# GLA scores prepared two levels at a time, and four more visits ahead of the gate rows' transposes, in a hybrid encoder layer on one core

## Chip, cores and metric

The kernel runs on one core of one Trainium2 chip. The metric is device time in microseconds (us), the median of several runs. PE is TensorE (PEld its weight loads), DVE is VectorE, ACT is ScalarE, POOL is GpSimd, SP is the engine that issues nearly all DMAs.

## What is computed

One layer of an encoder over 1024 tokens of width 1024. Token mixing normalises the input, projects it once, and gives the columns to two groups of four heads: mLSTM heads and GLA heads (linear attention with a forget gate for every key dimension). Both are scanned forward and backward and added, normalised per head, gated, projected out, normalised and added to the input. Then comes a gated MLP with a depthwise convolution of width 3. Cut to the part that the change touches, GLA in one direction is:

```
b = jnp.cumsum(a_, axis=-2)
diff = b[..., :, None, :] - b[..., None, :, :]
decay = jnp.exp(jnp.where(causal, diff, -jnp.inf))
s = jnp.einsum('bhtd,bhsd,bhtsd->bhts', q_, k_, decay)
o = jnp.einsum('bhts,bhse->bhte', s, v_) + jnp.einsum('bhtd,bhde->bhte', q_ * jnp.exp(b), s_st)
```

The scores s of two tokens need the decay between them, key dimension by key dimension, so they are no plain product of queries and keys.

## The kernel before

**Stages.** The input x is normalised, transposed and split into two parts (xh, xl) whose products keep fp32 accuracy. A first piece of the input projection runs at once (L259). Then two Python generators are interleaved: proj(), the rest of the input projection, and mix(), everything of the mixers. After them come the output projection (oacc, L957), the MLP (pr, L1018) and its down projection (pr, L1176), the last two by a Strassen scheme.

**The order of the work.** _interleave holds a clock for each generator and always advances the one whose clock is lower, up to its next yield, a visit. A visit adds the generator's weight to its clock. proj has 0.25. mix sets its own weight as it goes: W_AUX 0.85 at first, W_GLA 0.19, W_ML 0.26, W_OUT 0.5. So the weights and the yields decide how much projection stands between two pieces of the mixers. A visit of proj is 12 matmuls of 256 columns (t_block, L180, tile tacc) or 6 of 512 (f_block, L169, tile facc); proj has 176 such visits and a few without matmuls. The compiler then puts each engine's instructions in an order of its own: it keeps this order as priority, and takes a later instruction first where it reckons that the earlier one would wait.

**mix, in its order.** gla_decay (8 matmuls z, L374, and the cumulative gate sums, stored in dS); gate_rows, a generator that works out the gates of the mLSTM heads on DVE and ACT and ends in transposes of gi, gf and rm (tile ptc, L367) behind its last yield; gla(); mlstm(); out_weights(). gla waits with empty visits until the projections that it needs are done (done["bq"], done["bv"]), mlstm likewise for "aqk" and "av". gla runs levels(0), then states (the carried states of all 8 chunks), then for each chunk levels of the next one and finish of this one.

**levels(c)** makes the scores of one chunk of 128 tokens. It works by halving: for L = 64, 32, 16, 8, 4, 2, 1 the pairs of tokens that lie in the two halves of a block of 2L are given a reference point at the middle, so that the decay splits into a factor for the query and one for the key. For one L: POOL subtracts the reference (Dt, L610), ACT takes two exponentials into PSUM (E, L614 and L615), DVE multiplies them with the queries (Q, L624) and the keys (K, L628, or L622 for 32; for 64 a single product, L618). Then it yields, and in the next visit TensorE multiplies keys and queries (tile sc: L633 and L634 for 64, L645 for 32, L647 for the others), and the scores are kept: copied on ACT into Pt for 64 and 32 (L635, L636, L651), into acc for 16 (L653), and by DVE's copy_predicated into acc for the rest (L655). The diagonal (L661) follows in the same visit as L = 1, and then the operands of finish. That is 8 yields a chunk. D, E and Q have two buffers each, the pool ps, from which sc, the transposes and o are taken, has three banks.

**finish(c)** multiplies scores with values and adds the product with the state (tile o, L677, L678), copies it out and takes the norms on ACT.

**mlstm** takes matmuls Um (L729), sr (L753) and nd (L773, L774); the last nd is the last matmul of the mixers.

**out_weights** begins when mlstm has given back its memory. It loads the output weights in eight pieces of 512 KB (oraw, L817) through three buffers, two of tag yv and one of tag gv; each is split by ACT (woh, L106) and DVE (wol, L107), with a yield behind each. Once the projection is done (done["gate"]) it calls prep(0): the loads yv and gv of the first 128 tokens into the same buffers, their scaling on DVE (L837), transposes (L843) and a split into yh and yl. The first output product (oacc, L957) needs the split weights and yh.

Of the kernel before, what the change touches and what calls it, by code (L numbers as in the profile page):

```python
# [9 lines left out]
F32 = mybir.dt.float32  # L10
F32R = mybir.dt.float32r
U32 = mybir.dt.uint32
AF = mybir.ActivationFunctionType
ALU = mybir.AluOpType
# [3 lines left out]
P = 128  # L18
# [5 lines left out]
H = 4  # L24
# [9 lines left out]
TEMP = 16.0  # L34
# [21 lines left out]
def tile_encoder_layer(  # L56
# [6 lines left out]
    nc = tc.nc  # L63
# [30 lines left out]
    ps = ps_ctx.enter_context(tc.tile_pool(name="ps", bufs=3, space=PSUM))  # L94
# [28 lines left out]
    # ------------------------------------------------------------------  # L123
    # normalised input, transposed and split
    # ------------------------------------------------------------------
# [33 lines left out]
    bmask = mid.tile([P, 5, 32], U32, name="bmask")  # L159
    # ------------------------------------------------------------------  # L160
    # input projection
    # ------------------------------------------------------------------
# [87 lines left out]
    for t in range(NT):  # L250
# [5 lines left out]
        acc = mm.tile([P, NS], F32, name="vacc", tag="mm")  # L256
# [3 lines left out]
        if t % 4 == 0:  # L260
            vst = stg.tile([P, 4, 256], F32, name="stg")
        nc.scalar.copy(out=sml[:, t, 0:96].rearrange("p (n r) -> p n r", n=3),
                       in_=acc[:, 256:288].rearrange("p (o r) -> p o r", o=1).broadcast_to([P, 3, 32]))
# [35 lines left out]
    def gate_rows():  # L299
# [7 lines left out]
        for i in range(2):  # L307
            rs = slice(32 * i, 32 * i + 4)
# [20 lines left out]
        for i in range(2):  # L329
            rs = slice(32 * i, 32 * i + 4)  # L330
# [6 lines left out]
        for i in range(2):  # L337
            rs = slice(32 * i, 32 * i + 4)
# [24 lines left out]
        yield  # L363
# [122 lines left out]
    # ------------------------------------------------------------------  # L486
    # mixers and the rest of the input projection
    # ------------------------------------------------------------------
    mctx = ExitStack()

    def mix():
# [49 lines left out]
        def gla():  # L541
# [51 lines left out]
            def levels(c):  # L593
# [11 lines left out]
                mi = 0  # L605
                for L in (64, 32, 16, 8, 4, 2, 1):
                    nb = P // (2 * L)
                    Dt = w2k("D")
                    xv = X.rearrange("p h (n j) -> p h n j", j=2 * L)
                    nc.gpsimd.tensor_tensor(out=Dt.rearrange("p h (n j) -> p h n j", j=2 * L), in0=xv,  # L610
                                            in1=xv[:, :, :, L:L + 1].broadcast_to([P, H, nb, 2 * L]), op=ALU.subtract)
                    E = pe.tile([P, H, P], F32, name="E", tag="pe")
                    half = lambda z, i: z.rearrange("p h (n i j) -> p (h n) i j", i=2, j=L)[:, :, i, :]
                    nc.scalar.activation(half(E, 0), half(Dt, 0), AF.Exp, scale=-1.0 / TEMP)  # L614
                    nc.scalar.activation(half(E, 1), half(Dt, 1), AF.Exp, scale=1.0 / TEMP)  # L615
                    Q = w2k("Q")
                    if L == 64:
                        nc.vector.tensor_tensor(out=Q, in0=E, in1=z64, op=ALU.mult)  # L618
                    elif L == 32:
                        nc.vector.tensor_tensor(out=Q, in0=E, in1=qq, op=ALU.mult)  # L620
                        K = w2k("K", 1)
                        nc.vector.tensor_tensor(out=K, in0=E, in1=kk, op=ALU.mult)  # L622
                    else:
                        nc.vector.tensor_tensor(out=Q, in0=E, in1=qq, op=ALU.mult)  # L624
                        K = kz[L]
                        for i in range(2):
                            rs = slice(64 * i, 64 * i + 64)
                            nc.vector.tensor_tensor(out=half(K[rs], i), in0=half(E[rs], i), in1=half(kk[rs], i), op=ALU.mult)  # L628
                    yield
                    if L == 64:  # L630
                        sc = ps.tile([P, H, 64], F32, name="sc", tag="ps")
                        for h in range(H):
                            nc.tensor.matmul(sc[0:64, h, :], Q[0:64, h, 0:64], Q[0:64, h, 64:128], start=True, stop=True)  # L633
                            nc.tensor.matmul(sc[64:128, h, :], Q[64:128, h, 64:128], Q[64:128, h, 0:64], start=True, stop=True)  # L634
                        nc.scalar.copy(out=Pt[0:64, :, 64:128], in_=sc[0:64])  # L635
                        nc.scalar.copy(out=Pt[64:128, :, 0:64], in_=sc[64:128])  # L636
                    else:
                        sc = ps.tile([P, H, 32], F32, name="sc", tag="ps")
                        for h in range(H):
                            for b in range(4):  # L640
                                bs = slice(32 * b, 32 * b + 32)
                                if L == 32:
                                    ob = slice(32 * (b ^ 1), 32 * (b ^ 1) + 32)
                                    rs = lo if b % 2 == 0 else hi
                                    nc.tensor.matmul(sc[bs, h, :], K[rs, h, bs], Q[rs, h, ob], start=True, stop=True)  # L645
                                else:
                                    nc.tensor.matmul(sc[bs, h, :], K[:, h, bs], Q[:, h, bs], start=True, stop=True)  # L647
                        if L == 32:
                            for b in range(4):
                                ob = slice(32 * (b ^ 1), 32 * (b ^ 1) + 32)  # L650
                                nc.scalar.copy(out=Pt[32 * b:32 * b + 32, :, ob], in_=sc[32 * b:32 * b + 32])  # L651
                        elif L == 16:
                            nc.scalar.copy(out=acc, in_=sc)  # L653
                        else:
                            nc.vector.copy_predicated(acc, bmask[:, mi:mi + 1, :].broadcast_to([P, H, 32]), sc)  # L655
                            mi += 1
                sc = ps.tile([P, H, 32], F32, name="sc", tag="ps")
                for h in range(H):
                    for b in range(4):
                        bs = slice(32 * b, 32 * b + 32)  # L660
                        nc.tensor.matmul(sc[bs, h, :], kk[:, h, bs], qq[:, h, bs], start=True, stop=True)  # L661
                nc.vector.copy_predicated(acc, bmask[:, mi:mi + 1, :].broadcast_to([P, H, 32]), sc)
# [202 lines left out]
    # ------------------------------------------------------------------  # L865
    # output projection, norms, residual; operands of the gated MLP
    # ------------------------------------------------------------------
# [159 lines left out]
    # ------------------------------------------------------------------  # L1027
    # gated MLP
    # ------------------------------------------------------------------
# [89 lines left out]
    # ------------------------------------------------------------------  # L1119
    # down projection, norm and residual  # L1120
    # ------------------------------------------------------------------
# [148 lines left out]
```

## Times and profile before

| | |
|---|---|
| runs | 1217.5, 1218.92, 1219.08 us |
| median | 1218.92 us |
| span of the profiled execution (no time of its own is given beside it) | 1217.3 us |
| PE busy | 1186.4 us (97%) |
| DVE busy | 902.5 us (74%) |
| ACT busy | 601.0 us (49%) |
| POOL busy | 128.1 us (11%) |

How to read it: a line of the waits names the engine, tile and line that waited, what it waited for, and then the total, the number and the longest of the waits in us. A line of the timeline has the start, the duration, the engine, the line, the operation, out<-in, the shapes and the count, and in brackets the idle time before it and what ended it. A line of the windows has the stretch, its length, busy time and count of instructions (in brackets) of the engines in the order PE, PEld, DVE, ACT, POOL (or of the first two, where one line is asked for), then the granted TensorE clock, the share of the DMA engines and GB/s. Durations of matmuls overlap, since they are pipelined; the distance of two starts says how fast they go.

### The profile page before, as it was taken

To read this page: it belongs to the slowest core of one execution; us is meant where nothing else is said; L and a number is where in the kernel's file an instruction comes from. 1 tells how busy PE (TensorE), PEld (TensorE's weight loads), DVE (VectorE), ACT (ScalarE), POOL (GpSimd) and SP (SyncE) were. 2 spreads that over 40 slices of the span, in tenths; PEclk is the share of its full clock that TensorE was granted. 3 is DMA by queue.
4 is the path that set the end of the run, shared out by engine and by line. 5 is a ranking of instruction groups with operands and counts; after the bars stand their busy time and mean duration, and the time that the engine had idled before them with its cause. 6 is when DMAs were issued, how large, how long until landed. Compare 5 with 4: busy or idle time off the path is not lost.

```text
span 1217.3 us, 21301 instructions
## 1 busy us (share of the span) xinstructions
PE 1186.4 (97%) x7896; PEld 994.7 (82%) x7896; DVE 902.5 (74%) x1644; ACT 601.0 (49%) x1326; POOL 128.1 (11%) x167
## 2 busy tenths in 40 slices
PE   8998999999999999999999999999999999999997
PEld 7988778888888898887788888888888878888886
DVE  6586689677455556667998887888787867977667
ACT  6562777777545543545643333333332335445542
POOL 1201333554000100011000000000000000000001
PEclk9998999999999999999999999999999999999999
DMA  7453675453666467532143322423133319854345
GB/s 210 132 140 92 194 212 142 141 158 118 179 178 157 156 205 243 189 139 96 35 139 121 122 80 93 130 95 123 51 121 113 113 63 317 264 153 149 94 131 189
DMA packets 134652, 175.77 MB, mean 144 GB/s; under 512 B 24965, under 2 KB 89861, under 8 KB 134549
## 3 DMA queue, kind: packets, MB, share of 16 engines
q1 hardware_dynamic: 134116, 172.58, 45.9%
q0 software_dynamic: 432, 1.84, 0.4%
q8 instruction: 62, 1.02, 0.3%
q14 instruction: 42, 0.34, 0.1%
HBM read 126.78 MB, written 47.53 MB: 143 GB/s over the span
## 4 chain that ended last, share of the span: by engine, by line
PE 73%; DVE 2%; ACT 1%; DMA 1%; issue 1%; POOL 0%; DVEq 0%; POOLq 0%; ACTq 0%
PE pr L1018 35%; PE pr L1176 17%; PE tacc L180 8%; PE oacc L957 6%; PE nd L774 2%; PE nd L773 2%; PE sr L753 1%; PE Um L729 1%; PE pt L843 0%; PE sc L647 0%; PE pt L935 0%; DMA v<-dva 0%; DMA yv<-dya 0%; DVE xr L978 0%; ACT sq L535 0%
## 5 line engine op out<-in xcount | busy, mean ns | idle before, releaser
L1018 PE MATMUL pr<-T,ah 128*128 128x512 f32 x704 | 222.1, 397 | 1.1 <-DVE G L1056 1.1
L1018 PE MATMUL pr<-B,ah 128*128 128x512 f32 x528 | 164.3, 392 | 0.0
L1018 PEld LDWEIGHTS pr<-T,ah 128*128 128x128 f32 x704 | 132.4, 188 | 33.4 <-DVE G L1056 1.5
L1018 PE MATMUL pr<-T,al 128*128 128x512 f32 x352 | 139.5, 396 | 0.0
L180 PE MATMUL tacc<-wh,xh 128*128 128x256 f32 x448 | 131.5, 293 | 0.0
L180 PE MATMUL tacc<-wl,xh 128*128 128x256 f32 x448 | 129.9, 290 | 0.0
L180 PE MATMUL tacc<-wh,xl 128*128 128x256 f32 x448 | 129.6, 289 | 0.0
L1176 PE MATMUL pr<-dwl,dah 128*128 128x512 f32 x308 | 120.0, 390 | 0.7 <-DVE dwl L111 0.7
L1176 PE MATMUL pr<-dwh,dal 128*128 128x512 f32 x308 | 120.1, 390 | 0.0
L1176 PE MATMUL pr<-dwh,dah 128*128 128x512 f32 x308 | 119.0, 389 | 0.0
L1018 PEld LDWEIGHTS pr<-B,ah 128*128 128x128 f32 x528 | 99.1, 188 | 22.3
L1018 PE MATMUL pr<-B,al 128*128 128x512 f32 x264 | 103.4, 392 | 0.0
L110 ACT CAST dah<-ar 128x512 fp32r<-128x512 f32 x77 | 47.8, 622 | 98.0 <-PE pr L1176 51.3
L180 PEld LDWEIGHTS tacc<-wh,xh 128*128 128x128 f32 x448 | 86.9, 194 | 2.4
L180 PEld LDWEIGHTS tacc<-wl,xh 128*128 128x128 f32 x448 | 87.0, 194 | 1.1
L180 PEld LDWEIGHTS tacc<-wh,xl 128*128 128x128 f32 x448 | 86.9, 194 | 0.9
L110 ACT CAST ah<-fraw 128x512 fp32r<-128x512 f32 x64 | 39.6, 619 | 86.1 <-PE pr L1018 56.3
L111 DVE TENSOR_TENSOR dal<-ar,dah 128x512 fp32r<-128x512 f32 x77 | 53.0, 689 | 36.9 <-ACT dah L110 36.9
L1018 PEld LDWEIGHTS pr<-T,al 128*128 128x128 f32 x352 | 66.3, 188 | 16.1
L110 ACT CAST ah<-sa 128x512 fp32r<-128x512 f32 x44 | 27.3, 621 | 87.5 <-PE pr L1018 53.4
L1176 PEld LDWEIGHTS pr<-dwl,dah 128*128 128x128 f32 x308 | 57.8, 188 | 13.1 <-DVE dwl L111 1.1
L1176 PEld LDWEIGHTS pr<-dwh,dal 128*128 128x128 f32 x308 | 57.8, 188 | 12.5 <-DVE dal L111 0.6
(293 smaller groups left out, 2565.7 us busy)
## 6 DMA issues: line engine op xcount, KB each, us to landing
ar<-dA SPq DMA_DIRECT2D x77, 256.0 KB
wraw<-in_w_in_dram SPq DMA_DIRECT2D x48, 256.0 KB
fraw<-in_ffn_w_gate_dram SPq DMA_DIRECT2D x22, 512.0 KB
fraw<-in_ffn_w_up_dram SPq DMA_DIRECT2D x22, 512.0 KB
dA<-s SPq DMA_DIRECT2D x20, 512.0 KB
dA<-sx SPq DMA_DIRECT2D x10, 768.0 KB
Y<-in_ffn_w_down_dram SPq DMA_DIRECT2D x22, 256.0 KB
S<-dS SPq DMA_DIRECT2D x16, 258.0 KB
```

The costliest lines, as they stand in the source:

```text
L110: nc.scalar.copy(out=hi, in_=src)
L111: nc.vector.tensor_tensor(out=lo, in0=src, in1=hi.bitcast(F32), op=ALU.subtract)
L180: nc.tensor.matmul(acc[:, i, :], v[:, k, ts], w[:, k, :], start=(k == 0 and n == 0), stop=(k == NK - 1 and n == 2))
L729: nc.tensor.matmul(U[:, j, 0:P + 1], KT[:, 2 * g + j, :], v[:, 2 * g + j, :], start=True, stop=True)
L753: nc.tensor.matmul(sr[:, h, :], kk[:, h, :], qq[0:64, h, :], start=True, stop=True)
L773: nc.tensor.matmul(nd[:, j, 0:P + 1], Ps[i][:, h, :], v[:, h, :], start=True, stop=False)
L774: nc.tensor.matmul(nd[:, j, 0:P + 1], RI[rs, h, :], mslots[rs, c, h, :], start=False, stop=True)
L957: nc.tensor.matmul(accs[hf], v[:, j, :], w[:, k, hf * 512:(hf + 1) * 512], start=(k == 0 and n == 0), stop=(k == NK - 1 and n == 2))
L1018: nc.tensor.matmul(acc, A[i][:, k, :], B[b][j][:, k, :], start=(k == 0 and n == 0), stop=(k == 3 and n == 2))
L1176: nc.tensor.matmul(accs[i], o[v][:, ts], o[w], start=(p == 0 and n == 0), stop=(p == NP - 1 and n == 2))
```

## The change

levels is taken apart into weigh (POOL, ACT and DVE work of one level), pair_up (the products) and keep. Levels go in pairs: both are weighed, with a yield behind each, then TensorE gets the products of both, then both are kept. The diagonal is a level 0 without weighing, and has a yield of its own, so there are 9 yields a chunk with the last one. In gate_rows the one yield ahead of the transposes becomes five. No operation is added or removed. The rest of the diff blanks out comment lines.

```
-        yield
+        for _ in range(5):
+            yield
         for c in range(NC):
             pt = ps.tile([P, 3, 36], F32, name="ptc", tag="ps")
...
-                mi = 0
-                for L in (64, 32, 16, 8, 4, 2, 1):
-                    nb = P // (2 * L)
+                half = lambda z, i, L: z.rearrange("p h (n i j) -> p (h n) i j", i=2, j=L)[:, :, i, :]
+
+                def weigh(L):
                     Dt = w2k("D")
...
-                    Q = w2k("Q")
+                    Q, K = w2k("Q"), None
                     if L == 64:
                         nc.vector.tensor_tensor(out=Q, in0=E, in1=z64, op=ALU.mult)
...
+                        return Q, K
+                    nc.vector.tensor_tensor(out=Q, in0=E, in1=qq, op=ALU.mult)
...
+                            nc.vector.tensor_tensor(out=half(K[rs], i, L), in0=half(E[rs], i, L), in1=half(kk[rs], i, L), op=ALU.mult)
+                    return Q, K
+
+                def pair_up(L, Q, K):
+                    sc = ps.tile([P, H, 64 if L == 64 else 32], F32, name="sc", tag="ps")
+                    for h in range(H):
...
+                    return sc
+
+                def keep(L, sc):
+                    if L == 64:
                         nc.scalar.copy(out=Pt[0:64, :, 64:128], in_=sc[0:64])
                         nc.scalar.copy(out=Pt[64:128, :, 0:64], in_=sc[64:128])
...
+                        mi = (8, 4, 2, 1, 0).index(L)
+                        nc.vector.copy_predicated(acc, bmask[:, mi:mi + 1, :].broadcast_to([P, H, 32]), sc)
+
+                for pair in ((64, 32), (16, 8), (4, 2), (1, 0)):
+                    ready_qk = []
+                    for L in pair:
+                        ready_qk.append(weigh(L) if L else (qq, kk))
+                        yield
+                    scs = [pair_up(L, *qk) for L, qk in zip(pair, ready_qk)]
+                    for L, sc in zip(pair, scs):
+                        keep(L, sc)
                 for b in range(4):
                     bs = slice(32 * b, 32 * b + 32)
                     nc.scalar.copy(out=Pt[bs, :, bs], in_=acc[bs])
```

More of the change, by code (lines that the diff above doesn't have):

```diff
@@ L610, in levels @@
                     nc.gpsimd.tensor_tensor(out=Dt.rearrange("p h (n j) -> p h n j", j=2 * L), in0=xv,
-                                            in1=xv[:, :, :, L:L + 1].broadcast_to([P, H, nb, 2 * L]), op=ALU.subtract)
+                                            in1=xv[:, :, :, L:L + 1].broadcast_to([P, H, P // (2 * L), 2 * L]), op=ALU.subtract)
                     E = pe.tile([P, H, P], F32, name="E", tag="pe")
-                    half = lambda z, i: z.rearrange("p h (n i j) -> p (h n) i j", i=2, j=L)[:, :, i, :]
-                    nc.scalar.activation(half(E, 0), half(Dt, 0), AF.Exp, scale=-1.0 / TEMP)
-                    nc.scalar.activation(half(E, 1), half(Dt, 1), AF.Exp, scale=1.0 / TEMP)
-                    Q = w2k("Q")
+                    nc.scalar.activation(half(E, 0, L), half(Dt, 0, L), AF.Exp, scale=-1.0 / TEMP)
+                    nc.scalar.activation(half(E, 1, L), half(Dt, 1, L), AF.Exp, scale=1.0 / TEMP)
+                    Q, K = w2k("Q"), None
                     if L == 64:
                         nc.vector.tensor_tensor(out=Q, in0=E, in1=z64, op=ALU.mult)
-                    elif L == 32:
-                        nc.vector.tensor_tensor(out=Q, in0=E, in1=qq, op=ALU.mult)
+                        return Q, K
+                    nc.vector.tensor_tensor(out=Q, in0=E, in1=qq, op=ALU.mult)
+                    if L == 32:
                         K = w2k("K", 1)
@@ L623, in levels @@
                     else:
-                        nc.vector.tensor_tensor(out=Q, in0=E, in1=qq, op=ALU.mult)
                         K = kz[L]
@@ L627, in levels @@
                             rs = slice(64 * i, 64 * i + 64)
[L628 to L632, printed above, removed]
+                            nc.vector.tensor_tensor(out=half(K[rs], i, L), in0=half(E[rs], i, L), in1=half(kk[rs], i, L), op=ALU.mult)
@@ L633, in levels @@
+                    return Q, K
[3 more added lines that the diff above has]
+                        if L == 64:
                             nc.tensor.matmul(sc[0:64, h, :], Q[0:64, h, 0:64], Q[0:64, h, 64:128], start=True, stop=True)
                             nc.tensor.matmul(sc[64:128, h, :], Q[64:128, h, 64:128], Q[64:128, h, 0:64], start=True, stop=True)
+                            continue
+                        for b in range(4):
+                            bs = slice(32 * b, 32 * b + 32)
+                            if L == 32:
+                                ob = slice(32 * (b ^ 1), 32 * (b ^ 1) + 32)
+                                rs = lo if b % 2 == 0 else hi
+                                nc.tensor.matmul(sc[bs, h, :], K[rs, h, bs], Q[rs, h, ob], start=True, stop=True)
+                            else:
+                                nc.tensor.matmul(sc[bs, h, :], K[:, h, bs], Q[:, h, bs], start=True, stop=True)
+                    return sc
@@ L635, in levels @@
+                def keep(L, sc):
+                    if L == 64:
                         nc.scalar.copy(out=Pt[0:64, :, 64:128], in_=sc[0:64])
                         nc.scalar.copy(out=Pt[64:128, :, 0:64], in_=sc[64:128])
-                    else:
[L638 to L662, printed above, removed]
+                    elif L == 32:
+                        for b in range(4):
+                            ob = slice(32 * (b ^ 1), 32 * (b ^ 1) + 32)
+                            nc.scalar.copy(out=Pt[32 * b:32 * b + 32, :, ob], in_=sc[32 * b:32 * b + 32])
+                    elif L == 16:
+                        nc.scalar.copy(out=acc, in_=sc)
+                    else:
+                        mi = (8, 4, 2, 1, 0).index(L)
+                        nc.vector.copy_predicated(acc, bmask[:, mi:mi + 1, :].broadcast_to([P, H, 32]), sc)
```

## The prediction

> **What bounds the kernel now.** I read the page's busy times first, then TensorE's waits, then the windows of the projection's matmuls, and only then single instructions. One line each of the page (span, busy time of the engines):
>
> ```profile
> span 1217.3 us, 21301 instructions
> PE 1186.4 (97%) x7896; PEld 994.7 (82%) x7896; DVE 902.5 (74%) x1644; ACT 601.0 (49%) x1326; POOL 128.1 (11%) x167
> ```
>
> TensorE is busy for 1186.4 of 1217.3 us. The change adds and removes no operation, so its time can only come out of, or go into, the 31 us in which TensorE does nothing, and the time that its matmuls lose to switches and to a lower granted clock. The waits of TensorE (total, times, longest, in us):
>
> ```profile
> PE sc L647 <- DVE kz L628: 6.3, 7, 1.3
> PE ptc L367 <- DVE gf L355: 4.2, 1, 4.2
> PE sc L645 <- DVE K L622: 1.3, 1, 1.3
> PE sc L647 <- issue: 1.0, 1, 1.0
> ```
>
> 12.8 us of the 31 lie in the two places that the change touches: 8.6 us at the GLA score products (L645, L647) and 4.2 us at the gate rows' transposes (ptc). Both are filled with projection. So I ask where that projection is taken from. The windows of L180 (tacc, 12 matmuls a visit of proj) and, second, of L169 (facc, 6 a visit); the first number in brackets is the count of matmuls:
>
> ```profile
> 85.50:103.95 18.45, 10.15 (x84) 10.21 (x84) 1.00 0.43 114
> 345.10:431.90 86.80, 27.43 (x197) 24.18 (x195) 1.00 0.52 148
> 431.90:464.00 32.10, 31.57 (x261) 31.36 (x261) 1.00 0.69 238
> ...
> 0.00:85.50 85.50, 36.75 (x156) 29.35 (x157) 0.98 0.57 159
> 85.50:103.95 18.45, 8.39 (x37) 6.65 (x36) 1.00 0.43 114
> ```
>
> The order of the work is a count that can be done by hand from _interleave: proj adds 0.25 to its clock at each visit, mix adds 0.85, 0.19, 0.26 or 0.5. So a visit of mix brings 3.4 visits of proj up to the gate rows, 0.76 in GLA, 1.04 in the mLSTM heads, 2 in out_weights. Proj has 176 visits with matmuls. My count for the code of before gives 39 ahead of ptc; the rows give (156+37)/6 + 84/12 = 39.2. It gives 16 during the mLSTM chunks (345 to 432 us); the row gives 197/12 = 16.4. It gives 22 left when mix reaches out_weights; the row from 431.90 gives 261/12 = 21.8. In between the order on TensorE runs some visits ahead of the count, because the compiler fills what it expects to be waits, but it comes back to it. The last 31.6 us of projection are a cover: nothing but the loading and splitting of w_out (out_weights) and prep(0) runs beside them.
>
> **The change part by part.**
>
> **1. Five yields ahead of ptc.** Four more visits of mix at 3.4 are 13.6 visits of proj, 12 or 13 of them with matmuls: at 12 x 0.12 us = 1.44 us (spacing of tacc in the rows under 2) some 18 us of work. ptc waited 4.2 us for gf; the chain to gf runs on DVE and ACT and gets no longer, and 18 us more in front of ptc cover the wait four times. It goes: 4.2 us. It also cost clock. Windows behind the wait, all engines (counts of PE first, PEclk third from the end):
>
> ```profile
> 112.00:114.00 2.00, 2.00 (x12) 1.93 (x11) 0.00 (x0) 0.50 (x2) 1.46 (x3) 0.50 0.72 207
> 114.00:116.00 2.00, 2.00 (x11) 2.00 (x11) 0.05 (x1) 1.10 (x2) 1.96 (x5) 0.50 0.17 57
> 116.00:118.00 2.00, 2.00 (x12) 2.00 (x11) 0.64 (x1) 0.00 (x0) 0.00 (x0) 0.50 0.81 268
> 118.00:120.00 2.00, 2.00 (x18) 2.00 (x18) 0.00 (x0) 0.00 (x0) 0.00 (x0) 0.99 0.70 189
> 177.00:304.00 127.00, 118.30 (x2346) 106.08 (x2345) 99.04 (x221) 94.73 (x275) 61.60 (x58) 1.00 0.49 142
> ```
>
> From 112 to 118 us 35 matmuls ran where at x18 per 2 us 54 fit: 35/9 = 3.9 us of work took 6.0, so 2.1 us are lost. The transposes just ahead of them ran at a low clock too; I add 0.9 for them (an estimate, between nothing and half of their 3 us) and take 3.0. Part 1 is worth -7.2 us (bounds -4.2 and -7.8). What is late next there is the same as before: the first GLA loads behind ptc, covered by projection that runs ahead.
>
> **2. Fewer switches.** One score visit between projection matmuls, and two score groups side by side (PE, start and duration):
>
> ```profile
> 217.24 0.28 PE L180 MATMUL tacc<-wl,xh 128*128 128x256 f32 x1
> 217.45 0.46 PE L647 MATMUL sc<-Q,kz 128*32 128x32 f32 x32
> 217.77 0.46 PE L661 MATMUL sc<-qq,kk 128*32 128x32 f32 x32
> 218.16 0.38 PE L677 MATMUL o<-v,Pt 128*128 128x128 f32 x1
> ...
> 229.16 0.28 PE L180 MATMUL tacc<-wl,xh 128*128 128x256 f32 x1
> 229.28 0.28 PE L180 MATMUL tacc<-wh,xl 128*128 128x256 f32 x1
> 229.49 0.46 PE L647 MATMUL sc<-Q,kz 128*32 128x32 f32 x32
> 229.88 0.39 PE L180 MATMUL tacc<-wh,xh 128*128 128x256 f32 x1
> ```
>
> A visit alone takes 229.88 - 229.28 = 0.60 us from one tacc to the next, 0.48 more than the spacing of 0.12. Two side by side take 218.16 - 217.24 = 0.92, 0.80 more. So a merge saves 2 x 0.48 - 0.80 = 0.16 us. Two such merges a chunk (16 with 8, 4 with 2) in 8 chunks: 2.6 us; 64 with 32 changes shape inside the pair, I give it 0.05 us x 8. Together -3.0 us (bounds 0, if the compiler's order already lays groups together, and -4).
>
> **3. The waits at the scores.** The DVE rows of one level:
>
> ```profile
> 245.06 0.69 DVE L624 TENSOR_TENSOR Q<-E,qq 128x512 f32<-128x512 f32 x1
> 245.66 0.41 DVE L628 TENSOR_TENSOR kz<-E,kk 64x256 f32<-64x256 f32 x1
> 246.00 0.28 DVE L655 COPY_PREDICATED acc<-bmask,sc 128x128 f32<-128x128 uint32 x1
> 246.31 0.43 DVE L628 TENSOR_TENSOR kz<-E,kk 64x256 f32<-64x256 f32 x1
> 246.77 0.69 DVE L624 TENSOR_TENSOR Q<-E,qq 128x512 f32<-128x512 f32 x1
> ```
>
> A level costs DVE 246.77 - 245.06 = 1.71 us, a pair 3.4. Q has two buffers, and now both are held until the pair's products have read them, so the next pair's first product on DVE starts behind them: I add 0.5 us, some 3.9 us a pair. TensorE has, between two pairs, two visits of mix = 1.52 of proj = 2.2 us and 0.9 us of scores, 3.1 us. So DVE sets the pace in a pair as it did for a level (1.71 against 1.1 + 0.6), and the difference is filled by projection running ahead, as in the trace. On the other hand products now come in 32 visits instead of 56, which can each be late, with more work in front of each pair. Bounds: all 8.6 us gone, or 8 us more (8 chunks at 1 us, the size of one wait today). I take half of them gone, -4 us. No clock comes back with it: the row 177 to 304 us grants 1.00 in spite of these waits.
>
> **4. What the projection does not cover any more.** This is what sets my sign. The same count for the changed code: four visits more in the gate rows and one more in each of 8 chunks (levels yields 9 times a chunk now, not 8: what falls to four is the visits with products) take 18 visits of proj forward, and only 4 are left when mix reaches out_weights: 4 x 1.44 = 5.8 us of cover instead of 31.6. What ran beneath it:
>
> ```profile
> 431.54 0.49 PE L774 MATMUL nd<-mslots,RI 64*128 64x129 f32 x2
> ...
> 434.17 1.36 SPq L817 DMA_DIRECT2D oraw<-in_w_out_dram  x3
> 440.47 0.33 SPq L817 DMA_DIRECT2D oraw<-in_w_out_dram  x1
> 456.77 0.32 SPq L833 DMA_DIRECT2D gv<-dG  x1
> ...
> 437.91 1.15 ACT L106 ACTIVATE woh<-oraw,hg 128x1024 fp32r<-128x1024 f32 x1 [2.56 <-DMA oraw<-in_w_out_dram]
> 444.02 1.15 ACT L106 ACTIVATE woh<-oraw,hg 128x1024 fp32r<-128x1024 f32 x1 [0.83 <-DMA oraw<-in_w_out_dram]
> ...
> 439.15 1.29 DVE L107 SCALAR_TENSOR_TENSOR wol<-oraw,hg,woh 128x1024 fp32r<-128x1024 f32 x1 [3.08 <-ACT woh L106]
> 461.93 2.19 DVE L837 SCALAR_TENSOR_TENSOR yv<-gv,hr,yv 128x128 f32<-128x128 f32 x8 [2.82 <-DMA gv<-dG]
> ...
> 463.36 1.15 PE L843 MATMUL pt<-ident,yv 128*128 128x128 f32 x8
> 464.68 0.73 PE L957 MATMUL oacc<-woh,yh 128*128 128x512 f32 x2 [0.18 <-ACT yh L110]
> ```
>
> The chain from the end of the last nd (432.0) to the first oacc (464.68) takes 32.7 us today and hides behind 31.6 us of projection with hardly a gap. It is a ring: w_out comes in eight pieces through three slots, prep(0) uses the same slots after them. Worked out without what delays it today: 2.2 us to the first issue (434.17); 3.7 us to the first piece (437.91); ACT 1.15 and DVE 1.29 until the slot is free (440.44); the next piece of that slot is issued at 440.47 and taken up at 444.02, so a round is 6.1 us, and the slot sees two more of them (to 452.6); then prep(0)'s load (3.6 us, as the piece of 440.47), half of the 2.19 us of scaling, transposes and split 1.3 (463.36 to 464.68): 26.7 us in all. What makes it 32.7 today are evacuations of projection on ACT and DVE between the pieces and a gv that is only issued at 456.77; most of that projection is gone by then. I take 28, near the lower end (bounds 26.7 and 32.7). TensorE stands for 28 - 5.8 = 22.2 us (bounds 20.9 and 26.9). There is nothing else for it: the first output product needs all of this, and the MLP's products need the output projection.
>
> Behind it the clock is low again, as behind ptc: 2.1 us of loss (bounds 1 and 4). The Trainium skill ("TensorE: Matmul & The Clock Gate", part 1, "What's actually happening") states that TensorE falls to half speed after an idle window of about 3.4 us and comes back after a busy one as long; by it the loss would be about 1.7 us (an estimate from that page), and the short score waits would cost no clock at all, which the rows above bear out. So the rule speaks against the change: it trades waits that are too short to lower the clock for one that is not.
>
> Sum: -7.2 - 3.0 - 4.0 + 22.2 + 2.1 = +10.1 us. The profiled span is 1217.3, the median of the three runs 1218.92 (1217.5 to 1219.08); I let the 1.6 us between them stand: **1229 us**.
>
> **The rivals.**
>
> A, the cover stays, faster: the order on TensorE leaves 20 visits for out_weights all the same, or the loads of w_out move ahead of the last nd. Then parts 1 to 3 stand alone: 1218.9 - 14.2 = 1204.7 us. For it: on TensorE projection does run ahead of the count, so the order is not fixed. Against it: at three places, the last one above all, the count is met within a visit. It decides the sign from a cover of 11 visits on (28 - 16 leaves 12 us, which parts 1 to 3 outweigh), or from a chain under 18 us; three rounds of 6.1 us alone are more. Chance 0.10.
>
> B, DVE paces the pairs and the order does not fill the gap: 0.8 us (3.9 - 3.1) at each of 24 pair boundaries is 19 us in place of the 4 gained. Part 4 unchanged, 1229 + 4 + 19 = 1252; half of it, 1240. For it: the waits of today are of that kind, up to 1.3 us. Against it: of the 40 product groups at L647 (five in each of 8 chunks) only 7 wait for DVE. Chance 0.13.
>
> C, no change: parts 1 to 3 at their best (-7.8 - 4 - 8.6) against part 4 at its least (20.9 + 1): +1.5 us, 1220. Chance 0.12.
>
> **How the numbers follow.** The forecast, a new stand of 20 to 27 us at w_out that outweighs the gains, has 0.65: with its terms near their bounds it gives 1221 to 1241. The range reaches over C and the lower half of B, 1217 to 1243, and leaves out A and the rest of B. What a measurement of this kernel tells from no change is 0.2%, 2.4 us. Faster takes A and a bit of C, 0.12; within 0.2% most of C and the low edge of the forecast, 0.12; slower 0.76.
>
> **What would show it.** In the profile after: no wait of ptc on gf and no half clock around it; score groups in pairs with 0.33 us from the start of one to the next; about 48 tacc matmuls behind the last nd instead of 261; then a wait of TensorE of some 20 us that ends in yv or yh ahead of the first oacc, with the clock at 0.50 behind it. It is wrong if more than 150 tacc matmuls stand behind the last nd, if the first piece of w_out is issued well before the last nd, or if the waits at L647's successors grow beyond 15 us.

## The result, and the profile after

The changed kernel takes 1232.74 us (median of four runs, 1232.66 to 1234.89) against 1218.21 us before (four runs, 1216.54 to 1219.08): a ratio of 1.0127, with an interval of 1.0108 to 1.0147. It is slower by 14.5 us. The forecast was 1229. Two executions that were disturbed as a whole, 4001.89 us in e7 and 1234.11 us in e8, are left out of the comparisons, and e7's profile, which fell into the first of them, is not read.

The page of the changed kernel, span and busy times:

```profile
span 1230.9 us, 21295 instructions
PE 1181.6 (96%) x7896; PEld 989.4 (80%) x7896; DVE 907.1 (74%) x1644; ACT 601.1 (49%) x1326; POOL 128.7 (10%) x167
```

TensorE issues the same 7896 matmuls and is busy for 4.8 us less than before, in a span that is 13.6 us longer. So its matmuls run a little better, and it stands still for 18 us more. The waits of TensorE in the changed kernel (total, times, longest, in us) say where:

```profile
PE pt L850 <- DVE yv L844: 22.2, 1, 22.2
PE sc L645 <- DVE kz L628: 4.9, 7, 1.1
PE sc L635 <- DVE Q L618: 2.6, 2, 2.3
...
PE U L585 <- ACT KT L581: 1.4, 2, 0.8
...
PE ptk L579 <- DVE Q L575: 0.5, 1, 0.5
PE sc L643 <- DVE K L623: 0.4, 1, 0.4
```

The 4.2 us of ptc on gf are gone, and one wait of 22.2 us for yv has come. Around it, the chain of waits in order of time (start, length, what), from the first load of w_out to the scaling of the first tokens:

```profile
447.83 5.02 DMA oraw<-in_w_out_dram
...
452.94 1.16 ACT woh L106
...
454.17 1.30 DVE wol L107
...
455.49 4.11 DMA oraw<-in_w_out_dram
...
462.12 4.65 DMA oraw<-in_w_out_dram
...
469.28 3.63 DMA yv<-dya
...
473.03 2.20 DVE yv L844 x8
```

This is the ring of out_weights: load, high half on ACT, low half on DVE, then the next load into the same slot, three times over, and after it prep(0) (the load of yv and its scaling). How much projection lay over it is seen in the window of L180 from the end of the last nd to behind the first oacc (time, PE busy and count of matmuls, PEld, PEclk, DMA share, GB/s):

```profile
444.90:476.00 31.10, 6.37 (x52) 6.16 (x52) 0.64 0.75 245
```

There are 52 projection matmuls, where 261 stood before. TensorE works for 6.37 of 31.10 us on them, and the mean clock there is 0.64. TensorE's rows at the end of the stand, and the windows behind it (all engines, PEclk third from the end):

```profile
473.44 2.12 PE L850 MATMUL pt<-ident,yv 128*128 128x128 f32 x7 [22.17 <-DVE yv L844]
475.38 0.80 PE L964 MATMUL oacc<-woh,yh 128*128 128x512 f32 x1
```

```profile
474.00:476.00 2.00, 2.00 (x8) 1.24 (x8) 1.86 (x6) 0.59 (x1) 0.00 (x0) 0.50 0.92 339
476.00:478.00 2.00, 2.00 (x8) 1.61 (x7) 0.74 (x2) 0.59 (x1) 0.00 (x0) 0.64 0.85 280
478.00:480.00 2.00, 2.00 (x10) 1.64 (x9) 1.17 (x5) 0.00 (x0) 0.00 (x0) 1.00 0.72 234
```

Because projection is only moved, a stage that has more of it gets longer without losing anything. So I keep a ledger. The span is cut at six marks: the first score product (first sc), the first mLSTM transpose (first ptm), the first score product of the mLSTM (first sr), the end of the last nd, the first oacc, the end. For each stretch I count the visits of proj in it (12 matmuls a tacc visit, 6 a facc visit), take off 1.44 us for each, and compare what is left with the kernel before. Two examples from the rows: before, (192 / 6 + 177 / 12) = 46.8 visits lie ahead of the first sc at 125.9 us, which leaves 58.5; after, 244 / 6 + 192 / 12 = 56.7 lie ahead of it at 131.1 us, which leaves 49.4. The changed kernel earns 9.1 us there. All kernels with a usable profile, in us against the profile of before:

| kernel | to sc | sc to ptm | ptm to sr | sr to nd | nd to oacc | oacc to end | sum |
|---|---|---|---|---|---|---|---|
| after | -9.1 | +0.1 | -3.3 | 0.0 | +22.9 | +2.9 | +13.6 |
| e1, gate yields only | -9.0 | +2.8 | -3.2 | 0.0 | +13.4 | +1.1 | +5.1 |
| e2, pairs only | -0.6 | +8.6 | -3.3 | -0.4 | +4.6 | +0.2 | +9.2 |
| e3, after, cover back | -7.7 | +4.6 | -1.0 | +2.9 | +1.1 | +4.6 | +4.5 |
| e4, before, cover gone | -1.0 | -1.8 | -2.9 | 0.0 | +22.9 | +2.6 | +19.8 |
| e5, pairs kept together | -9.0 | +3.1 | -3.1 | 0.0 | +22.3 | +8.4 | +21.6 |
| e6, after, cover from mLSTM | -7.9 | +0.2 | +3.0 | -0.1 | +10.0 | +0.9 | +6.1 |
| e8, gate yields, cover from mLSTM | -9.0 | +3.4 | -1.2 | -1.4 | +5.1 | +0.6 | -2.4 |
| e9, after, four slots | -8.7 | +0.1 | -2.9 | 0.0 | +19.4 | +1.9 | +9.8 |
| e10, gate yields, taken early | -2.2 | +6.3 | -1.3 | 0.0 | 0.0 | -0.1 | +2.7 |
| e11, e10 and four slots | -3.7 | +4.0 | -2.2 | 0.0 | 0.0 | +2.3 | +0.3 |
| e12, e8, four slots, GpSimd queue | -9.3 | +3.2 | -2.5 | +11.9 | +4.6 | -0.5 | +7.4 |

Each row is one profiled execution, and the same stage differs by some 2 to 3 us between kernels that are alike there. An entry of that size is read only where the waits or the clock of its stretch bear it out.

### The profile page after: what moved, and what is told of

Same layout as the page of the kernel before. It is cut to its first block, busy times and chain, and to the rows that moved or that the text cites. A ratio compares the mean times of both kernels' runs of the same rounds, so it can differ in the third digit from the quotient of the medians.

```text
span 1230.9 us, 21295 instructions
## 1 busy us (share of the span) xinstructions
PE 1181.6 (96%) x7896; PEld 989.4 (80%) x7896; DVE 907.1 (74%) x1644; ACT 601.1 (49%) x1326; POOL 128.7 (10%) x167
## 4 chain that ended last, share of the span: by engine, by line
PE 66%; DVE 7%; DMA 3%; ACT 3%; issue 1%; POOL 1%; DVEq 0%; POOLq 0%; SPq 0%; ACTq 0%
PE pr L1025 33%; PE pr L1183 15%; PE tacc L180 6%; PE oacc L964 4%; PE nd L781 2%; PE nd L780 2%; DMA oraw<-in_w_out_dram 1%; DMA yv<-dya 1%; DVE kz L628 1%; DMA gv<-dG 1%; DVE T L111 1%; PE sr L760 1%; DVE yv L844 1%; PE Um L736 1%; PE sc L645 0%
## 5 line engine op out<-in xcount | busy, mean ns | idle before, releaser
L180 PE MATMUL tacc<-wh,xh 128*128 128x256 f32 x448 | 130.4, 291 | 0.0
L180 PE MATMUL tacc<-wh,xl 128*128 128x256 f32 x448 | 128.2, 286 | 0.0
L180 PE MATMUL tacc<-wl,xh 128*128 128x256 f32 x448 | 128.2, 286 | 0.0
L1025 PEld LDWEIGHTS pr<-B,ah 128*128 128x128 f32 x528 | 99.1, 188 | 22.3
L180 PEld LDWEIGHTS tacc<-wh,xh 128*128 128x128 f32 x448 | 85.4, 191 | 2.2
L180 PEld LDWEIGHTS tacc<-wh,xl 128*128 128x128 f32 x448 | 85.5, 191 | 0.9
L180 PEld LDWEIGHTS tacc<-wl,xh 128*128 128x128 f32 x448 | 85.5, 191 | 0.6
L1183 PEld LDWEIGHTS pr<-dwh,dah 128*128 128x128 f32 x308 | 57.8, 188 | 12.8 <-ACT dah L110 0.8
```

Of the source, the lines that this page charges most:

```text
L180: nc.tensor.matmul(acc[:, i, :], v[:, k, ts], w[:, k, :], start=(k == 0 and n == 0), stop=(k == NK - 1 and n == 2))
L1025: nc.tensor.matmul(acc, A[i][:, k, :], B[b][j][:, k, :], start=(k == 0 and n == 0), stop=(k == 3 and n == 2))
L1183: nc.tensor.matmul(accs[i], o[v][:, ts], o[w], start=(p == 0 and n == 0), stop=(p == NP - 1 and n == 2))
```

## The experiments

**Theory:** the loss is the cover taken from w_out, whoever takes it; the gate rows and the pairs themselves earn a little. **Rivals:** the pairs lose time by themselves because DVE paces them; or the loads of w_out became slow for another reason.

**e4: the kernel before, with projection drawn forward by a weight.** Nothing of the change is in it.

```
-W_AUX, W_GLA, W_ML, W_OUT = 0.85, 0.19, 0.26, 0.5
+W_AUX, W_GLA, W_ML, W_OUT = 0.85, 0.24, 0.26, 0.5
```

> The kernel before with W_GLA 0.24 in place of 0.19, and nothing else: no pairs, no yields, but the count leaves only 3 visits (4.3 us). Theory: a wait of about 25 us ahead of the first oacc and 3 us of low clock, less what more projection saves in the mixers: 1240 to 1246 us. Rival: no change, 1218 us.

Measured: 1238.48 us (1237.11 to 1238.91), ratio 1.0163 (1.0148 to 1.0178), a little under the 1240 to 1246 expected. The wait of TensorE for yv in this kernel, and the window of its L180 matmuls from the last nd to the first oacc:

```profile
PE pt L843 <- DVE yv L837: 22.2, 1, 22.2
```

```profile
452.80:482.00 29.20, 4.96 (x40) 4.75 (x40) 0.64 0.79 249
```

The same 22.2 us stand there with the old levels and the old gate rows, and the ledger gives +22.9 and +2.6, where after has +22.9 and +2.9. This carries the main theory: one number, and the cover is gone. Nor did the loads get slower as a whole: from the last nd to the first oacc it is 30.5 us in the changed kernel and 32.7 us before.

**e3: the changed kernel, with the cover given back by the same weight.**

```
-W_AUX, W_GLA, W_ML, W_OUT = 0.85, 0.19, 0.26, 0.5
+W_AUX, W_GLA, W_ML, W_OUT = 0.85, 0.15, 0.26, 0.5
```

> The changed kernel with W_GLA 0.15 in place of 0.19, and nothing else: the count then leaves 21 visits (30 us) for the output weights, as before the change. Theory: the wait of 22 us ahead of the first oacc and the low clock behind it go, the gains stay: 1218 - 12 = about 1206 us, with waits at the scores up to 5 us longer because there is less projection between them. Rival (pairs cost by themselves): about 1230 us still.

Measured: 1221.48 us (1217.87 to 1225.89), ratio 1.0023 (1.0009 to 1.0036). The wait for yv falls from 22.2 to 1.0 us, and 11.3 of the 14.5 us come back. But 1206 us, which needed the gains of the other parts to stay, was missed. Two of its waits:

```profile
PE sc L645 <- DVE kz L628: 6.3, 6, 1.3
PE pr L1025 <- ACT oacc L971: 4.1, 1, 4.1
```

Projection that goes back to w_out is taken from between the scores, and GLA pays 4.6 us. The second row is a new wait of the first MLP product for the last output block, 4.1 us, which I did not foresee. e5 has it too, with no weight changed, so its cause is open. The visits of proj do not only cover w_out: in GLA too they are missed when they go.

**e1: the five gate yields alone**, with the old levels.

```
-        yield
+        for _ in range(5):
+            yield
```

> Only the five yields, levels as before. Theory (the time is set by how much projection is left to cover the loading of the output weights): the count leaves 10 visits, 14.4 us of cover for a chain of about 30 us, so TensorE waits some 15 us ahead of the first oacc; the waits at the gate rows and at the start of the mLSTM heads go (12 us). 1218 - 12 + 15 + 3 (low clock) = about 1224 us. Rival (the paired levels are what costs): no pairs here, so only the gain, about 1206 us.

Measured: 1225.97 us (1224.24 to 1227.47), ratio 1.0062 (1.0047 to 1.0077), as expected. Its wait for yv:

```profile
PE pt L844 <- DVE yv L838: 12.6, 1, 12.6
```

It earns 9.0 us ahead of the first sc, as the whole change does, and has 10 visits left at w_out, which leaves 12.6 us of the ring uncovered.

**e2: the pairs alone**, with a single yield in the gate rows.

```
-        for _ in range(5):
-            yield
+        yield
```

> Only the paired levels, one yield in the gate rows. Theory: the count leaves 17 visits, 24.5 us, so a wait of about 6 us ahead of the first oacc; the pairs themselves bring nothing, since the compiler's order takes their products apart again: 1222 to 1225 us, with the 4.2 us wait at ptc and its low clock still there. Rival (the pairs cost 14 us and more by themselves in the GLA stage): 1232 us or above, with the wait at the scores grown by 10 us.

Measured: 1227.14 us (1225.05 to 1229.34), ratio 1.0072 (1.0056 to 1.0088), some 2 us above what was expected. Its waits:

```profile
PE sc L644 <- DVE kz L627: 6.5, 6, 1.8
PE pt L849 <- DVE yv L843: 4.1, 2, 3.8
PE ptc L367 <- DVE gf L355: 3.8, 1, 3.8
PE sc L642 <- DVE K L622: 3.2, 1, 3.2
```

The wait for yv is 4.1 us, in line with the visits that eight more yields take. The ledger gives +8.6 us in GLA, where the whole change shows +0.1. The trace has two sources for it. From the first sc to the first ptm TensorE stands for 15.3 of 193.7 us; before, for 9.8 of 184.5. And the granted clock, 1.00 in all of that stretch before, falls twice, behind the wait of 3.2 us for K and behind a stand of 2.0 us ahead of o. The windows of all engines there:

```profile
188.00:192.00 4.00, 4.00 (x61) 2.82 (x48) 3.92 (x7) 1.66 (x7) 1.04 (x1) 0.57 0.15 29
226.00:230.00 4.00, 4.00 (x61) 3.53 (x60) 0.00 (x0) 1.36 (x4) 0.00 (x0) 0.59 0.21 64
```

At 0.57 and 0.59 these lose up to 1.7 and 1.6 us, which with 5.5 us more of standing makes 8.8. So the pairs alone are a loss there. Why the waits come out longer without the gate yields ahead of them (after against e1 is even -2.7) stays open.

**e5: the pairs forced to stay together on TensorE.** The compiler had taken them apart. TensorE's rows in the changed kernel, one pair (start, duration; of the projection matmuls between only the first and the last are shown):

```profile
219.49 0.46 PE L645 MATMUL sc<-Q,kz 128*32 128x32 f32 x32
219.88 0.39 PE L180 MATMUL tacc<-wh,xl 128*128 128x256 f32 x1
...
221.05 0.28 PE L180 MATMUL tacc<-wh,xl 128*128 128x256 f32 x1
221.26 0.46 PE L645 MATMUL sc<-Q,kz 128*32 128x32 f32 x32
```

The second group starts 1.77 us after the first, about the 1.71 us that DVE needs for a level, with ten projection matmuls between. Counted over GLA, TensorE has 49 separate stretches of scores, against 54 before and 32 if four a chunk were kept. The edit puts the first group of each pair behind the last instruction of the second:

```
-                    scs = [pair_up(L, *qk) for L, qk in zip(pair, ready_qk)]
+                    second = pair_up(pair[1], *ready_qk[1])
+                    with tc.issue_after(tc.nc.cur_bb.bb.instructions[-1]):
+                        first = pair_up(pair[0], *ready_qk[0])
+                    scs = [first, second]
```

> The changed kernel, with TensorE told to issue the products of a pair's first level right behind those of its second: 32 score groups on TensorE instead of the 49 of the changed kernel. Theory of the prediction (fewer switches, fewer places to wait): 3 us less for the switches and some 4 us less of waits, the GLA stage 3 to 7 us shorter than in the changed kernel, 1226 to 1230 us. Rival (DVE paces the pairs, and the Q buffers are held longer): waits at the scores grow, the GLA stage is 5 to 20 us longer, 1238 to 1252 us.

Measured: 1240.59 us (1238.11 to 1241.53), ratio 1.0177 (1.0162 to 1.0192), with 32 stretches: the rival's range, not the theory's. Waits of TensorE in this kernel between 135 and 324 us:

```profile
PE sc L645 <- DVE kz L628: 8.4, 14, 1.3
PE sc L643 <- DVE K L623: 2.3, 1, 2.3
PE ptk L579 <- DVE Q L575: 1.9, 3, 1.0
```

Pairs that really stay together wait for kz 14 times, not 7, and TensorE stands for 16.0 us of GLA, where the changed kernel has 10.5. DVE does pace them. This is the rival's mechanism, at 5.5 us of the 19 that I gave it. The ledger's GLA entry grows by less, 3.0 us, although 1.7 us of low clock come on top (0.72 from 198 to 204 us). So the fewer switches give back some 2.5 to 4 us, about what part 2 of the prediction had for them; it is a difference of single executions and no more than a sign. Most of the rest of its loss (+5.5 against after) lies behind the first oacc, at the same 4.1 us wait as in e3 and in the low clock behind it (0.57 from 584 to 592 us).

**e9: the changed kernel with a fourth slot in the ring.** gpost is loaded later, and its space serves the pieces of w_out.

```
-            raw = op.tile([P, D], F32, name="oraw", tag=("yv", "yv", "gv")[k % 3], bufs=(2, 2, 1)[k % 3])
+            raw = op.tile([P, D], F32, name="oraw", tag=("yv", "yv", "gv", "gpost")[k % 4], bufs=(2, 2, 1, 1)[k % 4])
```

> The changed kernel with four buffers for the pieces of the output weights instead of three (the buffer of gpost, loaded later, is the fourth), nothing else: two rounds of the ring instead of three. Theory (the exposed chain is the ring of loads and splits): one round of about 6 us less, so TensorE waits 16 us instead of 22 ahead of the first oacc, and 1226 to 1228 us. Rival (the loads are bound by the DMA engines, not by the ring): the wait stays at 20 to 22 us, 1231 us and above.

Measured: 1231.71 us (1228.93 to 1234.35), ratio 1.0112 (1.0091 to 1.0133). The wait falls from 22.2 to 19.4 us, not to the 16 expected, and the time is not clear of the changed kernel's. Its SP queue shows what held the rest:

```profile
448.56 0.88 SPq L823 DMA_DIRECT2D oraw<-in_w_out_dram  x2
453.38 0.38 SPq L479 DMA_DIRECT2D dG<-stg  x1
453.81 4.19 SPq L823 DMA_DIRECT2D oraw<-in_w_out_dram  x4
```

The queue goes in order. Behind two pieces stands the store of the last gate rows (dG), which waits for its evacuation; the third and fourth piece had free slots and waited behind it, some 4 us. The changed kernel's queue has the same gap (pieces at 447.83, dG at 452.65).

**e7: two gate yields** in place of one, old levels, to look for a middle.

```
-        yield
+        for _ in range(2):
+            yield
```

> The kernel before with two yields ahead of the gate rows' transposes instead of one: 3.4 visits, 4.9 us more projection there, just more than the wait of 4.2 us; 19 visits (27 us) are left for the output weights by the count. Theory: the wait and its low clock go (-5 to -9 us), the wait ahead of the first oacc is 2 to 4 us: 1211 to 1216 us. Rival (all five yields are needed): 1218 to 1221 us.

Measured: 1221.06 us (1219.58 to 1222.03), ratio 1.0024 (1.0014 to 1.0034). It missed 1211 to 1216 and lies in the rival's 1218 to 1221. There is no free gain in a smaller step; whether the wait of ptc went is not known, without a profile.

**e10: five gate yields, paid from ahead of the gate rows** (e1, and W_AUX 0.65 for 0.85), so that w_out keeps its cover.

```
-W_AUX, W_GLA, W_ML, W_OUT = 0.85, 0.19, 0.26, 0.5
+W_AUX, W_GLA, W_ML, W_OUT = 0.65, 0.19, 0.26, 0.5
```

> The kernel before with five yields ahead of the gate rows' transposes and W_AUX 0.65 in place of 0.85: the projection for them is taken from gla_decay, just ahead, and not from the end. By the count 41 visits stand ahead of ptc (39 before) and 22 are left for the output weights, as before. Theory: the wait of 4.2 us at ptc shrinks to 1 or 2 us with the clock staying up, nothing else changes: 1212 to 1216 us. Rival (DVE works on the gate chain until 108 us whatever stands beside it, so the wait only comes in another place): 1217 to 1220 us.

Measured: 1219.41 us (1214.0 to 1221.8), ratio 1.0005 (0.9992 to 1.0017), where the rival had 1217 to 1220. The profile is of the longest of its executions. The wait of ptc is gone and another stands behind it, at the first scores:

```profile
PE sc L634 <- DVE Q L619: 4.0, 1, 4.0
```

So the 9 us of part 1 are not the yields' doing. DVE's chain through the gate rows to the first Q has a length of its own; ten more visits of projection fill it, and yields without visits only push the wait on. The +6.3 in GLA is 14.7 us of standing, where before has 9.8, and a low clock behind this wait (0.57 from 124 to 128 us, 1.7 us).

**e6 and e8: the cover paid from the mLSTM heads.** e6 is the changed kernel with W_ML 0.15 for 0.26, e8 is e1 with W_ML 0.18.

```
-W_AUX, W_GLA, W_ML, W_OUT = 0.85, 0.19, 0.26, 0.5
+W_AUX, W_GLA, W_ML, W_OUT = 0.85, 0.19, 0.15, 0.5
```

> The changed kernel with W_ML 0.15 in place of 0.26, nothing else: the projection for the output weights (20 visits, 29 us, by the count) is taken from the mLSTM stage and not from GLA. Theory: what counts is how much is left at the end; TensorE's wait ahead of the first oacc is 0 to 3 us, the gain of 9 us at the gate rows stays, GLA keeps its 80 visits and with them its time: 1207 to 1213 us. Rival (each stage needs the projection that it had): the mLSTM stage stalls by 10 us or more, 1218 us and above.

> The kernel before with the five yields and W_ML 0.18 in place of 0.26, levels as before: 21 visits are left by the count. Theory: -9 us at the gate rows, +3 in GLA as in the run with the five yields alone, -2 at the start of the mLSTM heads, no wait ahead of the first oacc: 1208 to 1213 us, and by comparison with the run of the changed kernel with W_ML 0.15 the pairs are worth 0 to 3 us. Rival (the mLSTM stage stalls without its projection): 1218 us and above.

Both missed what was expected of them (1207 to 1213 and 1208 to 1213). Measured: e6 1232.52 us (1222.15 to 1237.46), ratio 1.0101 (1.0069 to 1.0133); its profiled execution, of span 1223.4, has only 14 visits left at w_out, not the 20 of the count, because the order on TensorE runs ahead of it, and waits for 9.2 us. e8 comes nearest to a gain: 1216.75 us (seven of ten runs 1214.4 to 1216.9, three 1227.1 to 1234.1), ratio 1.0004 (0.9973 to 1.0035). Its wait for yv:

```profile
PE pt L844 <- DVE yv L838: 4.4, 1, 4.4
```

With fewer visits between, the time is not stable from run to run, and it goes with the mean granted clock of the run: in e6 from 0.991 at 1222.15 us to 0.979 at 1237.46 us, in e8 0.993 to 0.995 in the seven runs and 0.984 and 0.982 at 1227.09 and 1228.62 us. Where in the kernel the clock was lost in those runs was not seen; e12, whose five runs have 0.980 to 0.985, shows one place.

**e11 and e12: four slots where the cover is whole, and e8 with four slots and the loads of w_out issued by GpSimd,** whose queue dG doesn't stand in. e11 is e10 with e9's edit; e12 is e8 with e9's edit and

```
-            nc.sync.dma_start(raw, w_out[:, k, :])
+            nc.gpsimd.dma_start(raw, w_out[:, k, :])
```

> The same as the run with W_AUX 0.65, and four buffers for the output weights. Theory: with 22 visits left the chain is covered either way, so the shorter ring brings nothing but less contention at the start of the output projection: 0 to 2 us below that run. Rival (the ring still costs there): 4 us or more below it.

> The run with the five yields and W_ML 0.18 (levels as before), with two more edits at the output weights: four buffers for the pieces, and their loads issued by GpSimd instead of SP, so that no store of the gates stands in front of them in the queue. Theory (the exposed chain is the ring, lengthened by SP's order): the 5 us that its stretch from the last nd to the first oacc is above that of the kernel before fall to 0 to 2 us, and the time is 1210 to 1214 us, below both kernels. Rival (that stretch is set by the DMA engines and by what the mLSTM stage left): no change against that run, 1216 to 1218 us.

Measured: e11 1219.49 us (1216.19 to 1227.68), ratio 1.0017 (1.0 to 1.0033): where the ring is covered, its length is worth nothing. e12 1229.95 us (1226.46 to 1232.2), ratio 1.0108 (1.0093 to 1.0124), far from the 1210 to 1214 expected. The stand at w_out is still +4.6 (from this queue a piece lands 3.8 to 7.7 us after its issue), and 11.9 us are lost in the mLSTM heads. One wait of TensorE there, and the windows of all engines around it:

```profile
PE nd L774 <- DVE RB L759: 2.0, 1, 2.0
```

```profile
350.00:355.00 5.00, 2.98 (x17) 2.17 (x17) 3.96 (x5) 3.99 (x11) 0.00 (x0) 1.00 0.55 179
355.00:360.00 5.00, 5.00 (x16) 3.51 (x15) 1.45 (x7) 0.62 (x2) 0.00 (x0) 0.54 0.19 52
360.00:380.00 20.00, 20.00 (x67) 15.04 (x66) 8.40 (x29) 7.01 (x27) 1.01 (x1) 0.50 0.42 95
380.00:385.00 5.00, 5.00 (x34) 5.00 (x34) 1.09 (x2) 1.29 (x5) 0.00 (x0) 0.73 0.95 204
```

A wait of 2.0 us is followed, some 3 us later, by 25 us at about clock 0.50, in which TensorE is busy all along. The projection's share of that stretch, of e12 and then of before (L180; time, PE, PEld, PEclk):

```profile
355.00:380.00 25.00, 3.13 (x11) 2.54 (x12) 0.51 0.37 86
```

```profile
355.00:380.00 25.00, 8.03 (x58) 7.21 (x59) 1.00 0.53 145
```

Half of 25 us is about 12 us; with the wait of 2.0 us that covers the whole entry of the ledger, 11.9. 58 projection matmuls stood in that stretch before, 11 stand in it now. So the filler seems to have one more use, to keep the clock up among small products; that is read from these rows, not tried by itself.

No version tried is faster than the kernel before by more than its interval.

## Why the prediction was right, and where it was not

The sign, the mechanism and the size of the largest term were right; parts 2 and 3 were wrong; two smaller terms were mis-sized.

**What bounds the kernel.** That time goes into standing, switches and a lower clock fits the rows: in GLA, standing and clock together make up e2's +8.6 and e10's +6.3. That the place from which projection is taken decides most of it is shown: e3, e4, e8 and e10 change one weight and move the time by 7 to 20 us against the same kernel without it.

**Part 1, gate rows: -7.2 forecast, -9.1 measured.** The wait on gf is gone. The size that was off is the clock: the windows of all engines, in before behind the wait, and in after from 104 to 121 us, where it would have stood:

```profile
108.00:118.00 10.00, 9.62 (x52) 8.97 (x53) 2.21 (x4) 3.77 (x12) 3.42 (x7) 0.50 0.39 113
```

```profile
104.00:121.00 17.00, 17.00 (x127) 16.00 (x126) 7.59 (x12) 7.39 (x12) 0.00 (x0) 1.00 0.49 141
```

A grant of 0.50 over 9.6 busy us is a loss of up to 4.8 us, not 3.0; with the wait of 4.2 that is up to 9.0. The cause was told too simply: e10 removes the same wait and earns 2.2 us, so it is the visits, not the yields, that pay.

**Parts 2 and 3, the scores: -7.0 forecast, +0.1 measured.** The step that failed is "A merge saves 2 x 0.48 - 0.80 = 0.16 us. Two such merges a chunk". There were hardly any merges in the changed kernel: 49 stretches, where before had 54 and the program has 32. I had named the bound (0, if the compiler's order decides) and took the other end. The price itself may have been right: e5, with 32 stretches, points to a saving of that size. For the waits, "I take half of them gone" failed too: those of GLA for scores, ptk and U are 10.2 us after, 9.4 before. e5 shows that a true pair waits more.

**Not foreseen: -3.3 us where the mLSTM heads begin.** e1, e2, e4, e5 and e9, which all draw projection forward, have some -3 too, so it belongs to no part of the change alone. In before, TensorE waits there for v, and the clock falls behind it. The wait, and windows of all engines, before and after:

```profile
PE Um L729 <- DMA v<-dva: 1.5, 1, 1.5
```

```profile
318.00:320.00 2.00, 1.16 (x8) 1.19 (x8) 0.04 (x1) 0.42 (x2) 0.00 (x0) 0.86 0.66 193
320.00:322.00 2.00, 2.00 (x11) 1.66 (x11) 1.56 (x6) 1.06 (x3) 0.00 (x0) 0.50 0.07 21
```

```profile
320.00:359.00 39.00, 39.00 (x324) 37.41 (x324) 26.04 (x73) 20.94 (x54) 0.00 (x0) 1.00 0.63 181
```

After, that wait is absent and the clock is whole. That the one brings the other is read from these rows, not tried by itself.

**Short waits and the clock.** The prediction took it that waits as short as those at the scores cost no clock. In the rows that it shows, and in all of GLA in the changed kernel, that is so (1.00). It is no rule: 1.5 us at Um in before, and waits of 2.5 us in e1 and 3.2 us in e2, are followed by half clock.

**Part 4, w_out: wait 22.2 forecast, 22.2 measured.** The count left 4 visits (48 matmuls); 52 stood there. That the wait agrees to the tenth is partly luck. The chain took 30.5 us from the end of the last nd (444.86) to the first oacc (475.38), not 28, because pieces took 4.1 to 5.0 us from issue to use, where I had 3.7 and 3.6 from before, and the first was issued 3.0 us behind the last nd, not 2.2. Why the pieces took longer is open: in before, too, three were under way when one took 3.7. The cover was 6.4 us, not 5.8, and the first transposes, 1.9 us of work (473.44 to 475.38), I had counted as stand: 30.5 - 6.4 - 1.9 = 22.2. The stretch costs 22.9 by the ledger. For the low clock I had 2.1 us; the windows give half of 473.4 to 476 and 0.36 of 476 to 478, 2.0 us, of which about 1 lies ahead of the first oacc. The other 1.9 of the +2.9 behind it are not accounted for; single executions differ by as much. e4 made the same stand with a weight, e3 took it away with a weight, and e9's shorter ring shortened it by 2.8 us: this cause is shown.

The sum was +10.1 against +13.6 in the profiled span. The gate rows came out 1.9 us better than forecast, the scores 7.1 worse, the mLSTM start 3.3 better, w_out with what lies behind it 1.5 worse (25.8 for 24.3): together +3.4, and 13.6 - 10.1 = 3.5.

**The rivals.** A (the cover stays) fell on 52 matmuls. B (DVE paces the pairs) exists, as e5 shows, at 3 to 5.5 us, and the compiler avoids it by splitting the pairs. C needed the gains of parts 2 and 3.

## What to carry to other kernels

When one stream fills the gaps of another, every added yield is a withdrawal: count how much of the filler is left at each later stretch that has nothing else, and price that stretch uncovered, before pricing the gap that you fill. Putting two steps together in the program does not put them together on the engine if the compiler orders by readiness; count the stretches in the trace first. To compare such kernels by stage, take the filler's own time out of each stretch, and set what is left against how long the engine stood there and how long its clock was low.

## What the runs showed of the hardware

In the changed kernel a wait of 2.31 us for Q in GLA, ended at 195.19 us with projection around it, is followed by a granted clock of 1.00 in every window up to 205 us. In e1 the same wait, 2.53 us long and ended at 194.47 us, also with projection around it, is followed by a low clock:

```profile
195.00:199.00 4.00, 4.00 (x57) 3.51 (x56) 3.30 (x7) 3.15 (x11) 2.08 (x2) 0.57 0.31 70
```

A mean of 0.57 over 4 us is 3.4 us at 0.50. The traces keep the clock's changes: in all kernels with a usable profile, before the end of the program, every low stretch lasts 3.41 us or a whole multiple of it (3.41 behind Um and 10.24 behind ptc in before, 23.89 at the stand of the changed kernel, 27.31 in e12). Counted back in such steps from the fall at 195.09 us, e1's wait (191.94 to 194.47) lies within one step, 191.68 to 195.09. Counted back from the changed kernel's fall at 453.56 us, a boundary at 194.15 cuts its wait (192.88 to 195.19) in two. So a wait of this length may cost a step of half clock or nothing, as it seems by where it falls among the steps; that is read from these two traces, not tried by itself.

Behind a wait of 2.0 us in e12 the granted clock stayed at about 0.50 from 355 to 380 us although TensorE was busy, with few projection matmuls among small ones, and came back in the window in which projection was dense again (34 matmuls from 380 to 385 us).

The Trainium skill ("TensorE: Matmul & The Clock Gate", part 1, "What's actually happening") has the clock fall after an idle window of about 3.4 us and return after a busy one as long. The length of the steps agrees with the traces, and so does the return behind the changed kernel's stand of 22.2 us: the transposes start at 473.44 and the clock is at 1.00 by 478. The fall does not need as long an idle time: it came 2.3 us after the last matmul ahead of that stand (451.27 to 453.56), and behind waits of 2.0 us in e12 and 2.53 us in e1. Nor does busy time always bring the clock back: 25 us of modelled busy time in e12 did not. What counts as busy, no run here separates.

Loads of 512 KB took 3.6 and 3.7 us from issue to use in before, in windows of DMA share 0.87 and 0.90 (440 to 442 and 434 to 438 us), and 4.1 to 5.0 us in the changed kernel, in a stretch of share 0.75; no run shows why. A store that waited in SP's queue held two loads behind it for some 4 us although their slots were free (e9).
